# A decoder layer on one core: front-stage DMAs on other queues, larger sample loads, repeated outputs copied from scratch

## The chip, the cores and the metric

The kernel runs on 1 core of one Trainium2 chip. The metric is the device time of one execution in microseconds, the median of three runs. The engines of the core work side by side, each through its own instructions in program order: TensorE (PE in the profile), VectorE (DVE), ScalarE (ACT), GpSimd (POOL) and SyncE (SP), which only issues DMAs here. Any engine but TensorE and VectorE issues DMAs in this kernel; what it issues is carried out by 16 DMA engines.

## The reference

One layer of a decoder, run for a prompt of 1024 tokens and for 8 sequences of 4 new tokens (1056 tokens in all), width 1024, all in float32:

```python
def trunk_layer(x, h0_re, h0_im, mem_k, mem_v, attend, ...):
    q, k, v, u = jnp.split(x @ w_in, [512, 1024, 1536], axis=-1)
    o_att = attend(q, k, v)                     # 8 heads of 64, dilated windows
    y_ssm, h_re, h_im = s5_mixer(u, h0_re, h0_im, ...)   # 32 groups of 16 channels, state 64
    mixed = jnp.concatenate([rms_norm(o_att, g_att), rms_norm(y_ssm, g_ssm)], -1) @ w_out
    x = layer_norm(alpha * x + mixed, ln1_g, ln1_b)
    x = layer_norm(alpha * x + memory_attention(x, mem_k, mem_v, w_mem_q, w_mem_o), ln2_g, ln2_b)
    ffn = (jax.nn.silu(x @ w_gate) * (x @ w_up)) @ w_down       # 2816 wide
    return layer_norm(alpha * x + ffn, ln3_g, ln3_b), k, v, h_re, h_im

# s5_mixer: h[l] = abar * h[l-1] + bbar u[l];  y = Re(C h) + D u;  g = gelu(y)
#           out = g * sigmoid(g @ w_glu + b_glu)
# attend, prompt: windows (128,1), (512,4), (2048,16), combined by their denominators
# attend, sample: the same over a cache of 1024 keys and values per sequence, then the new ones
# memory_attention: 4 heads of 256 over 256 memory tokens
```

Outputs are y of both token groups, the keys and values k and v, the last SSM states, and the keys and values of the memory tokens.

## The kernel before, in words

Products are made from float32 weights as three products of a high and a low part each. A strip of weights, 128 x 1024 or 512 KB, is loaded into a buffer `wraw` (two of them) by `fetch` (line 180), ScalarE casts it to its high part `whi` (L190), and VectorE makes the low part `wlo` by subtraction (L191); `fetch` is then called for the next strip. Tokens are worked in blocks of 384, 384 and 288.

The front stage is `project`. It makes strip after strip of the input projection: first u (the SSM's input), then q, k and last v in rows of 128 tokens (`gemm_v`, L427 to L429). ScalarE copies each result from PSUM into a buffer `stg` (three of them) and stores it to scratch in DRAM: `s_u`, `s_q`, `s_k`, `s_v`. Of k and v it stores each strip twice, to scratch and to the output (`kT`, `v`; `evac_k`, `evac_v`).

Between these strips two other pieces of work are placed. `ssm()` does the SSM in two halves of 16 groups (`qf`). A half has a preparation of tables `Bs` and `CA` (L1427 to L1429, VectorE for the real and GpSimd for the imaginary parts), a load of `U` from `s_u` in eight pieces (SyncE), tap matrices that go to scratch `s_kp` (four stores on SyncE) and come back as the tile `M` (tag `ET`, eight loads on GpSimd, L1472), matmuls into `HX` (L1467), a serial scan on VectorE (L1480 to L1484), fix-ups on both engines (L1496 to L1501), output matmuls (L1511 with `M`, L1515 with `CA` and `HX`) and a gelu (L1518) into `Y`, which uses the buffer of `Bs`. GpSimd stores the state from `HX` (L1520) and SyncE stores `Y` to `s_y` in eight pieces (L1523). `sample_attn` and `sample_finish` do the attention of the new tokens: SyncE loads the caches `ckT` and `cv` in steps of four 256 KB pieces into `skv` (eight buffers, L708); VectorE and TensorE use them (L774 the values, L780 the new values).

Behind `project`, `glu` loads `s_y` as `gT` (four loads, L496) and makes the gate matmuls; the attention of the prompt loads q, k and v back from scratch (`Vn`, `Vf`). Then come the output projection, the memory attention (`evac_mem` stores each strip of memory keys and values twice, on SyncE) and the feed-forward part (`gate_up`, whose `raw` loads weights on SyncE).

`between` calls the pieces in turn, but the order of each engine's instructions is set by a list scheduler at build time, which simulates a timeline; within an engine the order is then fixed.

Of the kernel before, what the change touches and what calls it, by code (L numbers as in the profile page):

```python
# [24 lines left out]
NC = 2  # L25
MO, GU = 50, 58
# [114 lines left out]
class Body:  # L141
# [33 lines left out]
    def fetch(self):  # L175
        i = self.w_f
        if i >= self.limit or i >= len(self.rows):
            return
        r = self.t(self.wp, [128, 1024], "wraw", bufs=2)
        self.nc.scalar.dma_start(r[:], self.a["wst"][self.rows[i]])  # L180
        self.w_raw[i] = r
        self.w_f += 1
# [58 lines left out]
    def body(self, st):  # L241
        self.st = st
        tc, nc, a = self.tc, self.nc, self.a
        self._n, self._c, self.todo = 0, {}, []
        self.limit = MO

        self.rows = list(range(MO + 8)) + list(range(MO, MO + 4)) + list(range(GU, GU + 2 * NC)) + list(range(DN, a["wst"].shape[0]))
        self.w, self.w_raw, self.w_f, self.w_s = {}, {}, 0, 0
        pool = lambda name, **kw: tc.tile_pool(name=name, bufs=1, **kw)
        self.cp = st.enter_context(pool("const"))  # L250
        self.wp = st.enter_context(pool("w"))
        self.ap_ = st.enter_context(pool("act"))
        self.pp = st.enter_context(pool("ps", space=PSUM))
        self.dp = st.enter_context(pool("dram", space=bass.MemoryType.DRAM))
        self.ident = self.t(self.cp, [128, 128], "ident")
        self.ones = self.t(self.cp, [128, 128], "ones")
        self.vecs = self.t(self.cp, [128, 60], "vecs")
        nc.vector.memset(self.ones[:], 1.0 / 1024)
        self.vhalf = self.t(self.cp, [128, 8], "vhalf")
        self.vneg = self.t(self.cp, [128, 60], "vneg")  # L260
        self.phase12(st)

    def phase12(self, st):
        tc, nc, a = self.tc, self.nc, self.a
        A = [self.unit("a0"), self.unit("a1")]
        xa = lambda b, k: (A[k // 4][b][0][:, k % 4, :], A[k // 4][b][1][:, k % 4, :])
        scr = lambda name, shape: self.dp.tile(shape, F32, name=name, tag=name)
        self.s_u = scr("s_u", [512, 8 * 144])
        self.s_y = scr("s_y", [512, 8 * 136])
        self.s_kp = scr("s_kp", [2, 16, 16, 240])  # L270
        self.s_q = scr("s_q", [512, 1024])
        self.s_k = scr("s_k", [512, T])
        self.s_v = scr("s_v", [T, 512])
        self.s_mk = scr("s_mk", [128, 2048])
        self.s_mv = scr("s_mv", [128, 2048])
        self.s_z = scr("s_z", [128, 8 * T])
        self.s_x1 = scr("s_x1", [128, 8 * T])
        self.s_h = {(f, b): scr(f"s_h{f}_{b}", [128, 2 * BLK[b][1]]) for f in range(NF // 2) for b in range(3)}
        self.qs = self.t(self.cp, [128, 4, 32], "qs")
        self.ks = self.t(self.cp, [128, 4, 32], "ks")  # L280
        self.os = self.t(self.cp, [128, 4, 32], "os")
        self.qsum = self.t(self.cp, [128, 32], "qsum")
        with tc.tile_pool(name="ostage", bufs=1) as og:
            self.project(A, xa, og)
        self.rest()

    def project(self, A, xa, og):
# [3 lines left out]
        def evac_q(n, b, ps):  # L291
# [5 lines left out]
            if b == 2:  # L297
                nc.scalar.activation(self.qs[:, n, :], ps[:, 256:288], AF.Copy, scale=0.125)
            nc.scalar.dma_start(self.s_q[n * 128:(n + 1) * 128, off:off + w], r[:, :w])

        def evac_k(n, b, ps):
# [3 lines left out]
            if b == 2:  # L305
                nc.scalar.copy(self.ks[:, n, :], ps[:, 256:288])
            for o in (self.s_k, a["kT"]):
                nc.scalar.dma_start(o[n * 128:(n + 1) * 128, off:off + w], r[:, :w])

        def evac_v(r, ch, ps):  # L310
            t_ = self.t(og, [128, 384], "stg", bufs=3)
            lo, row = (0, 128 * r) if r < 8 else (96, 1024)
            nc.scalar.copy(t_[lo:, :256], ps[lo:, :256])
            for o in (a["v"], self.s_v):
                nc.scalar.dma_start(o[row:row + 128 - lo, 256 * ch:256 * ch + 256], t_[lo:, :256])

# [5 lines left out]
        with tc.tile_pool(name="ps_a", bufs=1, space=PSUM) as self.pp2, tc.tile_pool(name="ssm_small", bufs=1) as self.sp, tc.tile_pool(name="ssm_part", bufs=1) as sh, \  # L322
# [30 lines left out]
            def evac_u(n, b, ps):  # L353
# [9 lines left out]
                if b == 2:  # L363
                    for d in (u[:, 0:4, 0:8], u[:, 4:8, 136:144]):
                        nc.scalar.copy(d.rearrange("p t b -> p b t"), ps[:, 256:288].rearrange("p (b t) -> p b t", t=4))
                    nc.scalar.dma_start(self.s_u[n * 128:(n + 1) * 128, :], u[:].rearrange("p s c -> p (s c)"))

# [21 lines left out]
            for _ in ssm:  # L389
                pass  # L390
        self.nps2 = 4
        self.pp2 = self.st.enter_context(tc.tile_pool(name="ps_b", bufs=1, space=PSUM))
# [53 lines left out]
    def evac_mem(self, o1, o2, c, ps, stage):  # L446
        r = self.t(stage, [128, 512], "stg", bufs=3)
        self.nc.scalar.copy(r[:, :256], ps[:, :256])
        for o in (o1, o2):
            self.nc.sync.dma_start(o[:, c:c + 256], r[:, :256])  # L450

# [38 lines left out]
    def glu(self):  # L490
        tc, nc, a = self.tc, self.nc, self.a
        with tc.tile_pool(name="glu", bufs=1) as gp:
            G, self.mix1 = self.unit("a0"), self.unit("a1")
            gT = self.t(gp, [128, 4, 8, 136], "gT")
            for n in range(4):
                nc.sync.dma_start(gT[:, n].rearrange("p t c -> p (t c)"), self.s_y[n * 128:(n + 1) * 128, :])  # L496
            src = []
# [200 lines left out]
    def sample_attn(self, ap):  # L698
# [6 lines left out]
        def load(src, gr, c):  # L705
            t_ = [self.t(ap, [128, 512], "skv", bufs=8) for _ in range(4)]
            for b4 in range(4):
                nc.sync.dma_start(t_[b4][:], a[src][4 * gr + b4, c])  # L708
            return t_

# [31 lines left out]
    def sample_finish(self, ap, probs, load, scores, masked, tsel, bsel):  # L742
# [15 lines left out]
        for gr, (S, nm, qb) in enumerate(probs):  # L758
# [12 lines left out]
            for c in range(5):  # L771
                vt = load("cv", gr, c)
                for b4 in range(4):
                    mm(po[32 * b4:32 * b4 + 32, :], PT[:, 128 * c + 32 * b4:128 * c + 32 * b4 + 32], vt[b4][:],  # L774
                       start=c == 0, stop=False)
                yield
            vs = self.t(ap, [128, 512], "skv", bufs=8)
            nc.sync.dma_start(vs[:32], self.s_v[1024:1056, :])
# [235 lines left out]
    def raw(self, f):  # L1014
# [4 lines left out]
        for i, r in enumerate(self.raws[f]):  # L1019
            self.nc.sync.dma_start(r[:], self.a["wst"][GU + 2 * f + i])  # L1020

# [314 lines left out]
    def ssm(self):  # L1336
# [73 lines left out]
        for qf in range(2):  # L1410
# [22 lines left out]
            for i in range(8):  # L1433
                nc.sync.dma_start(U[16 * i:16 * i + 16], su[:, 16 * qf:16 * qf + 16, 7 - i, :])
            for q in range(4):
# [18 lines left out]
            for j in range(4):  # L1454
                nc.sync.dma_start(self.s_kp[qf].rearrange("h (q j) x -> h q j x", j=4)[:, :, j, :],
                                  kp[32 * j:32 * j + 16].rearrange("p q n h -> p q (n h)"))
# [13 lines left out]
            M = H("ET", (128, 16, 128))  # L1470
            for i in range(8):
                g.dma_start(M[16 * i:16 * i + 16], self.s_kp[qf, :, :, 16 * i:16 * i + 128])  # L1472
            X = HX[:, :, :, 9:137].rearrange("p g r (J j) -> p g r J j", j=8)
# [46 lines left out]
            g.dma_start(a["st"][:, gs], HX[:, :, :, 136:145])  # L1520
            sy = self.s_y[:].rearrange("(g h) (t c) -> h g t c", h=16, t=8)
            for t_ in range(8):
                nc.sync.dma_start(sy[:, 16 * qf:16 * qf + 16, t_, :], Y[16 * t_:16 * t_ + 16])  # L1523

# [15 lines left out]
```

## Time and profile before

| | |
|---|---|
| three runs | 1684.59, 1692.92, 1695.85 us; median 1692.92 |
| the profiled execution | 1688.92 us |
| its span | 1687.2 us |
| mean granted TensorE clock, share of full speed | 0.975 |
| GpSimd's queue of DMAs | 2.25 MB, 0.8% of 16 engines' span |
| SyncE's and ScalarE's queues | 137.43 MB and 59.26 MB |

The span runs from the first to the last instruction that the profiler saw. An engine's busy time holds its computing instructions, and issues of DMAs only where a row names them. In the windows PEclk is the granted clock in parts of full speed, and the DMA share is that of 16 engines; it can pass 1 a little. In timelines a row ends with the idle time before it and what released it.

### The profile page before, as it was taken

Reading aid. Unit: us, or ns where it says so; the run is one execution under the profiler, and the core shown is the slowest. Engines: PE = TensorE matmul, PEld = TensorE weight load, DVE = VectorE, ACT = ScalarE, POOL = GpSimd, SP = SyncE. Lnnn points to the kernel's source line nnn. Section 1 sums busy time; section 2 is a strip of 40 time slices with the busy share of each in tenths; the row PEclk is TensorE's granted clock in tenths of the full one; section 3 lists DMA queues with packets and bytes.
Section 4 is the critical chain, followed back from the end, with each engine's and each line's share of the span. In section 5 each row is a group of like instructions: output and inputs, shape, how many; then the busy total and the mean of one; then the engine's idle time right before and its main releaser. Section 6 shows DMA issues by size and latency. Waiting matters only on the chain.

```text
span 1687.2 us, 27817 instructions
## 1 busy us (share of the span) xinstructions
PE 1605.1 (95%) x10910; PEld 1467.3 (87%) x10910; DVE 932.5 (55%) x1785; ACT 598.9 (35%) x1164; POOL 558.2 (33%) x568
## 2 busy tenths in 40 slices
PE   7999899899999988999998999999999999999996
PEld 7998765676677977987798989999999999999995
DVE  7555554366555886235537775555555545545545
ACT  5221221465434254235514543333333333211212
POOL 3423413032222644002126555444444441000134
PEclk9999999899999998999999999999999999999998
DMA  7547967713422365126620312222222224422301
GB/s 284 131 104 193 270 155 172 247 32 112 150 71 115 101 208 203 51 83 205 234 107 26 99 66 76 76 76 78 75 81 77 76 77 148 133 77 70 115 38 66
DMA packets 97683, 200.71 MB, mean 119 GB/s; under 512 B 10384, under 2 KB 52880, under 8 KB 96784
## 3 DMA queue, kind: packets, MB, share of 16 engines
q1 hardware_dynamic: 73456, 137.43, 25.8%
q10 hardware_dynamic: 23232, 59.26, 10.9%
q0 software_dynamic: 864, 2.25, 0.8%
q8 instruction: 86, 1.41, 0.4%
q14 instruction: 45, 0.37, 0.1%
HBM read 153.85 MB, written 45.04 MB: 118 GB/s over the span
## 4 chain that ended last, share of the span: by engine, by line
PE 77%; DMA 9%; DVE 6%; ACT 3%; issue 3%; POOL 2%; SPq 1%; ACTq 0%; POOLq 0%; DVEq 0%
PE g L1052 17%; PE g L209 12%; PE g L210 12%; PE g L211 12%; PE s L1052 7%; DMA wraw<-in_wst_dram 3%; PE s L596 2%; DMA skv<-in_cv_dram 2%; PE s L598 2%; DMA skv<-in_ckT_dram 1%; POOL z L857 1%; PE g L620 1%; DVE wlo L191 1%; PE q L774 1%; DMA hr<-s_h 1%
## 5 line engine op out<-in xcount | busy, mean ns | idle before, releaser
L209 PE MATMUL g<-a0h,whi 128*128 128x384 f32 (+1 forms) x768 | 254.3, 332 | 13.6 <-ACT whi L190 8.5
L211 PE MATMUL g<-a0h,wlo 128*128 128x384 f32 (+1 forms) x768 | 250.9, 327 | 4.6 <-DVE wlo L191 4.6
L210 PE MATMUL g<-a0l,whi 128*128 128x384 f32 (+1 forms) x768 | 252.0, 328 | 0.1
L209 PE MATMUL g<-a1h,whi 128*128 128x384 f32 (+1 forms) x672 | 221.3, 329 | 0.7 <-ACT a1h L335 0.7
L210 PE MATMUL g<-a1l,whi 128*128 128x384 f32 (+1 forms) x672 | 218.2, 325 | 2.8 <-DVE a1l L337 1.8
L211 PE MATMUL g<-a1h,wlo 128*128 128x384 f32 (+1 forms) x672 | 218.5, 325 | 0.0
L209 PEld LDWEIGHTS g<-a0h,whi 128*128 128x128 f32 x768 | 147.0, 191 | 20.7 <-ACT whi L190 8.7
L190 ACT CAST whi<-wraw 128x1024 fp32r<-128x1024 f32 x84 | 88.0, 1050 | 182.9 <-PE g L210 100.9
L211 PEld LDWEIGHTS g<-a0h,wlo 128*128 128x128 f32 x768 | 147.3, 192 | 6.2 <-DVE wlo L191 5.7
L210 PEld LDWEIGHTS g<-a0l,whi 128*128 128x128 f32 x768 | 147.3, 192 | 1.9 <-DVE a0l L511 0.7
L191 DVE TENSOR_TENSOR wlo<-wraw,whi 128x1024 fp32r<-128x1024 f32 x84 | 115.0, 1371 | 47.6 <-ACT whi L190 47.4
L209 PEld LDWEIGHTS g<-a1h,whi 128*128 128x128 f32 x672 | 128.4, 191 | 5.7 <-issue 3.1
L210 PEld LDWEIGHTS g<-a1l,whi 128*128 128x128 f32 x672 | 128.3, 191 | 3.7 <-DVE a1l L337 2.0
L211 PEld LDWEIGHTS g<-a1h,wlo 128*128 128x128 f32 x672 | 128.5, 191 | 0.4 <-issue 0.2
L1045 DVE TENSOR_TENSOR wlo<-wt,wlo 128x512 fp32r<-128x512 f32 x100 | 91.0, 911 | 26.5 <-ACT wlo L1044 24.7
L1044 ACT CAST wlo<-wt 128x512 fp32r<-128x512 f32 x100 | 62.0, 620 | 110.8 <-PE g L1052 89.4
L802 DVE TENSOR_TENSOR z<-z,g 128x384 f32<-128x384 f32 (+1 forms) x96 | 49.1, 518 | 90.0 <-PE g L211 89.8
L810 POOL TENSOR_TENSOR acc<-z 128x384 f32<-128x384 f32 (+1 forms) x6 | 8.5, 1412 | 186.4 <-DVE z L802 172.7
L608 POOL TENSOR_SCALAR S<-S,rD 128x128 f32<-128x128 f32 (+7 forms) x64 | 38.0, 599 | 85.3 <-DVE rD L607 54.5
L857 POOL TENSOR_SCALAR z<-z,vneg,vecs 128x384 f32<-128x384 f32 (+1 forms) x36 | 50.3, 1410 | 44.9 <-DVE z L853 44.9
L1220 POOL TENSOR_SCALAR S<-S,rD 128x256 f32<-128x256 f32 x32 | 15.2, 478 | 111.9 <-DVE rD L1209 106.1
L596 PE MATMUL s<-K,Q 64*128 64x256 f32 (+1 forms) x128 | 42.5, 442 | 5.9 <-DVE nm L604 5.9
(459 smaller groups left out, 4031.0 us busy)
## 6 DMA issues: line engine op xcount, KB each, us to landing
wraw<-in_wst_dram ACTq DMA_DIRECT2D x88, 512.0 KB, 4.0
skv<-in_ckT_dram SPq DMA_DIRECT2D x40, 256.0 KB, 4.8
skv<-in_cv_dram SPq DMA_DIRECT2D x40, 256.0 KB, 4.9
wraw<-in_wst_dram SPq DMA_DIRECT2D x20, 512.0 KB, 4.3
wru<-in_wst_dram SPq DMA_DIRECT2D x20, 512.0 KB, 4.3
hr<-s_h SPq DMA_DIRECT2D x22, 384.0 KB, 3.4
kvm<-in_cmk_dram SPq DMA_DIRECT2D x16, 512.0 KB, 4.8
wraw<-in_cmv_dram SPq DMA_DIRECT2D x16, 512.0 KB, 4.4
```

Source lines behind the costliest of these rows:

```text
L190: self.nc.scalar.copy(h[:], r[:])
L191: self.nc.vector.tensor_tensor(out=l[:], in0=r[:], in1=h[:], op=OP.subtract)
L209: mm(out, wh, xh, start=start, stop=False)
L210: mm(out, wh, xl, start=False, stop=False)
L211: mm(out, wl, xh, start=False, stop=stop)
L596: mm(ps[:, 32 * nf:w], q, k[:, 128 * max(qt - 1, 0):128 * qt + 128], start=True, stop=True)
L608: g.tensor_scalar(out=S[:, :w], in0=S[:, :w], scalar1=rD[:], scalar2=1.0, op0=OP.mult, op1=OP.mult)
L802: self.nc.vector.tensor_tensor(out=z[:, k], in0=z[:, k], in1=ps[:, :n], op=OP.add)
L857: g.tensor_scalar(out=z[:, k], in0=z[:, k], scalar1=sc, scalar2=bi, op0=OP.mult, op1=OP.add)
L1044: act.copy(t_[:, 0], src)
L1045: v.tensor_tensor(out=t_[:, 1], in0=src, in1=t_[:, 0], op=OP.subtract)
L1052: nc.tensor.matmul(ps[:, :n], p_, q_, start=first and k + j == 0, stop=k == 3 and j == 2, skip_group_check=not first)
```

## The change

Weight strips in `project`, the stores of `s_u`, `s_q`, `s_k` and `s_v`, the loads of `U` and the stores of `s_kp` are issued by GpSimd; from the end of `project` on, weights come by ScalarE's queue as before. SyncE loads a step of a sample cache with one DMA of 1 MB into one of two buffers. `M` is loaded by one DMA with an overlapping source pattern. `s_y` has another layout in scratch, is written by one DMA per half, and `gT` is read to match. The outputs `kT`, `v`, `memkT` and `memv` are no longer stored strip by strip; SyncE copies each from scratch by one DMA while `gate_up` runs, behind a weight load of the same step.

```diff
 project, start and end:
+        self.wq = nc.gpsimd
...
+        self.wq = nc.scalar
...
 fetch:
-        self.nc.scalar.dma_start(r[:], self.a["wst"][self.rows[i]])
+        self.wq.dma_start(r[:], self.a["wst"][self.rows[i]])
...
-        self.s_y = scr("s_y", [512, 8 * 136])
+        self.s_y = scr("s_y", [2, 16, 16, 8 * 136])
...
-            nc.scalar.dma_start(self.s_q[n * 128:(n + 1) * 128, off:off + w], r[:, :w])
+            nc.gpsimd.dma_start(self.s_q[n * 128:(n + 1) * 128, off:off + w], r[:, :w])
...
-            for o in (self.s_k, a["kT"]):
-                nc.scalar.dma_start(o[n * 128:(n + 1) * 128, off:off + w], r[:, :w])
+            nc.gpsimd.dma_start(self.s_k[n * 128:(n + 1) * 128, off:off + w], r[:, :w])
...
-            for o in (a["v"], self.s_v):
-                nc.scalar.dma_start(o[row:row + 128 - lo, 256 * ch:256 * ch + 256], t_[lo:, :256])
+            nc.gpsimd.dma_start(self.s_v[row:row + 128 - lo, 256 * ch:256 * ch + 256], t_[lo:, :256])
...
 evac_mem:
-        for o in (o1, o2):
-            self.nc.sync.dma_start(o[:, c:c + 256], r[:, :256])
+        self.nc.sync.dma_start(o2[:, c:c + 256], r[:, :256])
...
 glu:
-                nc.sync.dma_start(gT[:, n].rearrange("p t c -> p (t c)"), self.s_y[n * 128:(n + 1) * 128, :])
+                nc.sync.dma_start(gT[:, n],
+                                  self.s_y[n // 2, :, 8 * (n % 2):8 * (n % 2) + 8, :].rearrange("h g x -> g h x"))
...
 sample_attn, load:
-            t_ = [self.t(ap, [128, 512], "skv", bufs=8) for _ in range(4)]
-            for b4 in range(4):
-                nc.sync.dma_start(t_[b4][:], a[src][4 * gr + b4, c])
+            t_ = self.t(ap, [128, 4, 512], "skv", bufs=2)
+            nc.sync.dma_start(t_[:], a[src][4 * gr:4 * gr + 4, c].rearrange("b p n -> p b n"))
...
 raw:
+        again = {NC + 4: ("kT", self.s_k), NC + 7: ("v", self.s_v), NC + 10: ("memkT", self.s_mk), NC + 13: ("memv", self.s_mv)}.get(f)
+        if again:
+            with self.tc.issue_after(ins.ins):
+                self.nc.sync.dma_start(self.a[again[0]], again[1][:])
...
 ssm (g is gpsimd):
-                nc.sync.dma_start(U[16 * i:16 * i + 16], su[:, 16 * qf:16 * qf + 16, 7 - i, :])
+                g.dma_start(U[16 * i:16 * i + 16], su[:, 16 * qf:16 * qf + 16, 7 - i, :])
...
-                nc.sync.dma_start(self.s_kp[qf].rearrange("h (q j) x -> h q j x", j=4)[:, :, j, :],
+                g.dma_start(self.s_kp[qf].rearrange("h (q j) x -> h q j x", j=4)[:, :, j, :],
...
-            for i in range(8):
-                g.dma_start(M[16 * i:16 * i + 16], self.s_kp[qf, :, :, 16 * i:16 * i + 128])
+            taps = self.s_kp[qf]
+            taps = bass.AP(taps.tensor, taps.offset, [[16, 8], *[list(x) for x in taps.ap[:2]], [1, 128]])
+            g.dma_start(M[:], taps)
...
-            for t_ in range(8):
-                nc.sync.dma_start(sy[:, 16 * qf:16 * qf + 16, t_, :], Y[16 * t_:16 * t_ + 16])
+            nc.sync.dma_start(self.s_y[qf].rearrange("h g (t c) -> t (h g) c", t=8), Y[:])
```

GpSimd issues 94 DMAs in the front stage where it issued 18. This is GpSimd's order at the end of the second half's preparation before; `Bs` and `CA` are the tables, `p` their factors, `sS` belongs to the sample:

```order
L1427 TENSOR_TENSOR p_260_1897<-pw_650,bb_677 128x2x128
L1428 TENSOR_TENSOR p_261_1898<-pw_650,bb_677 128x2x128
L1429 TENSOR_TENSOR Bs_1845<-p_260_1897,p_261_1898 128x2x128
L1427 TENSOR_TENSOR p_260_1897<-pw_650,bc_586 128x288
L1428 TENSOR_TENSOR p_261_1898<-pw_650,bc_586 128x288
L1429 TENSOR_TENSOR CA_1846<-p_260_1897,p_261_1898 128x2x144
L1442 MEMSET Bs_2247 128x4x112
L755 TENSOR_SCALAR sS_1533<-sS_1533,srD_2388 128x672
L755 TENSOR_SCALAR sS_1950<-sS_1950,srD_2396 128x672
L1472 DMA ET_2482<-s_kp 16x16x128 x8
```

And the same place now, where `stg` is the buffer of a row of V:

```order
L1433 TENSOR_TENSOR CA_1796<-p_241_1831,p_242_1832 128x2x144
L314 DMA s_v<-stg_2340 32x256
L1431 TENSOR_TENSOR p_245_1847<-pw_650,bb_677 128x2x128
L1432 TENSOR_TENSOR p_246_1848<-pw_650,bb_677 128x2x128
L1433 TENSOR_TENSOR Bs_1795<-p_245_1847,p_246_1848 128x2x128
L314 DMA s_v<-stg_2586 128x256
L1431 TENSOR_TENSOR p_245_1847<-pw_650,bc_586 128x288
L1432 TENSOR_TENSOR p_246_1848<-pw_650,bc_586 128x288
L1433 TENSOR_TENSOR CA_1796<-p_245_1847,p_246_1848 128x2x144
L1446 MEMSET Bs_2162 128x4x112
L314 DMA s_v<-stg_2614 128x256
L1459 DMA s_kp<-Bs_2162 64x1x240 x4
L314 DMA s_v<-stg_2661 128x256
```

Three stores of V rows stand among the preparation's rows, more behind it, and the stores of the taps follow on the same engine. SyncE's order around the first half's store of `s_y` was this, with loads of `U` for the second half in between:

```order
L708 DMA skv_2069<-in_ckT_dram 128x512
L1434 DMA U_2214<-s_u 16x16x144 x3
L1523 DMA s_y<-Bs_1775 16x16x136 x8
L1434 DMA U_2214<-s_u 16x16x144
L708 DMA skv_2126<-in_ckT_dram 128x512
L708 DMA skv_2127<-in_ckT_dram 128x512
L708 DMA skv_2128<-in_ckT_dram 128x512
L708 DMA skv_2129<-in_ckT_dram 128x512
L1434 DMA U_2214<-s_u 16x16x144 x3
L708 DMA skv_2188<-in_ckT_dram 128x512
L708 DMA skv_2189<-in_ckT_dram 128x512
L708 DMA skv_2190<-in_ckT_dram 128x512
```

And is now:

```order
L707 DMA skv_1902<-in_ckT_dram 128x4x512
L707 DMA skv_1948<-in_ckT_dram 128x4x512
L707 DMA skv_2001<-in_ckT_dram 128x4x512
L1526 DMA s_y<-Bs_1732 8x256x136
L707 DMA skv_2054<-in_ckT_dram 128x4x512
L707 DMA skv_2109<-in_ckT_dram 128x4x512
L707 DMA skv_2630<-in_cv_dram 128x4x512
```

The loads of `U` are gone from it, and a step of the cache is one row.

## Rows read from the trace of the kernel before

**Rows 1.** The page: span, and busy time of each engine with its share

```profile
span 1687.2 us, 27817 instructions
...
PE 1605.1 (95%) x10910; PEld 1467.3 (87%) x10910; DVE 932.5 (55%) x1785; ACT 598.9 (35%) x1164; POOL 558.2 (33%) x568
```

**Rows 2.** Windows of the front, one row per stretch; us

```profile
core 0: us, PE busy (x) PEld busy (x) DVE busy (x) ACT busy (x) POOL busy (x), PEclk, DMA share, GB/s
137.00:152.00 15.00, 11.86 (x114) 10.58 (x111) 12.07 (x18) 1.84 (x3) 12.58 (x16) 0.96 1.04 173
273.00:289.00 16.00, 12.87 (x69) 6.75 (x66) 9.66 (x14) 2.57 (x4) 9.62 (x13) 1.00 0.99 157
314.00:333.00 19.00, 13.21 (x84) 9.03 (x83) 8.36 (x19) 10.85 (x21) 0.67 (x2) 0.79 1.05 371
333.00:345.00 12.00, 11.92 (x50) 10.28 (x49) 5.91 (x13) 6.12 (x14) 0.98 (x3) 0.63 0.31 105
```

**Rows 3.** DMA view, 137:152, then 273:289 us: KB, us to landing

```profile
out_dram<-HX POOLq DMA_DIRECT2D x1, 72.0 KB, 13.2
...
out_dram<-HX POOLq DMA_DIRECT2D x1, 72.0 KB, 16.2
```

**Rows 4.** Chain of waits, 270 to 345 us: start, us, what

```profile
274.90 13.77 DMA skv<-in_cv_dram
...
293.41 0.66 PE s L1511 x4
294.07 0.67 PE s L1515 x8
...
299.69 0.12 PE g L428
...
303.26 0.67 ACT Bs L1518 x2
...
309.30 4.49 DMA s_y<-Bs
...
326.31 6.02 DMA wraw<-in_wst_dram
...
333.23 0.32 PE g L209
```

**Rows 5.** Timeline of GpSimd: start, us, instruction, idle before and releaser

```profile
181.57 0.74 POOL L1429 TENSOR_TENSOR Bs<-p,p 128x256 f32<-128x256 f32 x1 [10.86 <-DMA out_dram<-stg]
...
226.80 4.49 POOL L1472 DMA_DIRECT2D ET<-s_kp  x8 [10.97 <-PE s L1467]
...
269.11 1.36 POOL L1496 TENSOR_TENSOR p<-HX,qw 128x210 f32<-128x210 f32 x2 [1.28 <-DVE HX L1484]
...
282.60 0.61 POOL L1501 TENSOR_TENSOR HX<-HX,p 128x210 f32<-128x210 f32 x1
```

**Rows 6.** Timeline of VectorE inside the second half's scan

```profile
262.09 0.69 DVE L782 TENSOR_TENSOR sS<-q,sm 128x512 f32<-128x512 f32 x1 [11.31 <-PE q L780]
```

**Rows 7.** GpSimd's M loads, line 1472: ns min/median/max, first and last start

```profile
L1472 POOL DMA_DIRECT2D ET<-s_kp x16: 562/564/769, 101.5 to 230.7; - x16
```

**Rows 8.** Timeline of ScalarE: two stores of one strip

```profile
237.81 0.34 ACTq L315 DMA_DIRECT2D out_dram<-stg  x1
241.61 0.33 ACTq L315 DMA_DIRECT2D s_v<-stg  x1
```

**Rows 9.** Timeline of SyncE: the issues of the second half's s_y

```profile
303.95 6.22 SPq L1523 DMA_DIRECT2D s_y<-Bs  x8
```

**Rows 10.** DMA view of the whole run: loads of V rows

```profile
Vn<-s_v SPq DMA_DIRECT2D x4, 512.0 KB, 6.6
```

**Rows 11.** Waits, 560 to 720 us: us in total, times, longest

```profile
ACT whi L190 <- DMA wraw<-in_wst_dram: 17.5, 9, 3.6
...
ACT stg L448 <- DMA s_mv<-stg: 3.6, 1, 3.6
```

**Rows 12.** Window in the middle of gate and up

```profile
1100.00:1200.00 100.00, 100.00 (x629) 100.00 (x628) 51.23 (x72) 37.28 (x71) 46.63 (x39) 1.00 0.24 79
```

More of the change, by code (lines that the diff above doesn't have):

```diff
@@ L365, in evac_u @@
                         nc.scalar.copy(d.rearrange("p t b -> p b t"), ps[:, 256:288].rearrange("p (b t) -> p b t", t=4))
-                    nc.scalar.dma_start(self.s_u[n * 128:(n + 1) * 128, :], u[:].rearrange("p s c -> p (s c)"))
+                    nc.gpsimd.dma_start(self.s_u[n * 128:(n + 1) * 128, :], u[:].rearrange("p s c -> p (s c)"))
             self.gemm_n(0, 4, xa, evac_u, group=2)
@@ L705, in load @@
         def load(src, gr, c):
-            t_ = [self.t(ap, [128, 512], "skv", bufs=8) for _ in range(4)]
-            for b4 in range(4):
-                nc.sync.dma_start(t_[b4][:], a[src][4 * gr + b4, c])
-            return t_
+            t_ = self.t(ap, [128, 4, 512], "skv", bufs=2)
+            nc.sync.dma_start(t_[:], a[src][4 * gr:4 * gr + 4, c].rearrange("b p n -> p b n"))
+            return [t_[:, b4] for b4 in range(4)]
         def scores(o, n, q, keys):
@@ L773, in sample_finish @@
                 for b4 in range(4):
-                    mm(po[32 * b4:32 * b4 + 32, :], PT[:, 128 * c + 32 * b4:128 * c + 32 * b4 + 32], vt[b4][:],
+                    mm(po[32 * b4:32 * b4 + 32, :], PT[:, 128 * c + 32 * b4:128 * c + 32 * b4 + 32], vt[b4],
                        start=c == 0, stop=False)
                 yield
-            vs = self.t(ap, [128, 512], "skv", bufs=8)
+            vs = self.t(ap, [128, 512], "skv", bufs=2)
             nc.sync.dma_start(vs[:32], self.s_v[1024:1056, :])
@@ L1019, in raw @@
         for i, r in enumerate(self.raws[f]):
-            self.nc.sync.dma_start(r[:], self.a["wst"][GU + 2 * f + i])
+            ins = self.nc.sync.dma_start(r[:], self.a["wst"][GU + 2 * f + i])
+        again = {NC + 4: ("kT", self.s_k), NC + 7: ("v", self.s_v), NC + 10: ("memkT", self.s_mk), NC + 13: ("memv", self.s_mv)}.get(f)
+        if again:
+            with self.tc.issue_after(ins.ins):
+                self.nc.sync.dma_start(self.a[again[0]], again[1][:])
     def gate_up(self, up, X, x2):
@@ L1520, in ssm @@
             g.dma_start(a["st"][:, gs], HX[:, :, :, 136:145])
-            sy = self.s_y[:].rearrange("(g h) (t c) -> h g t c", h=16, t=8)
-            for t_ in range(8):
-                nc.sync.dma_start(sy[:, 16 * qf:16 * qf + 16, t_, :], Y[16 * t_:16 * t_ + 16])
+            nc.sync.dma_start(self.s_y[qf].rearrange("h g (t c) -> t (h g) c", t=8), Y[:])
 def kernel(**inputs):
```

## The prediction

> **What bounds the kernel now.** I read the page first: TensorE is busy 1605.1 us of the span of 1687.2 us [rows 1], so all its gaps together come to 82 us, and a change to the front stage can win no more than those that lie there. Then the windows by stage: look at the share that the DMA engines are busy beside the rate they reach. At 137 to 152 us and at 273 to 289 us the share is 1.04 and 0.99 and the rate only 173 and 157 GB/s; at 314 to 333 us the same share carries 371 GB/s [rows 2]. The DMA view names what fills the slow windows: the store of the SSM state, 72 KB in runs of 36 bytes, lands after 13.2 and 16.2 us [rows 3]. The change leaves it alone.
>
> Then the chain of waits through the second part of the front [rows 4]. It shows a sample load of the cache as a link of 13.77 us that ends at 288.7; short matmuls of the SSM; a gelu at 303.26; the store of the SSM's output s_y, landed at 313.8; the load of V; a late weight strip; and a first GLU matmul at 333.23 that takes 0.32 us, since the granted clock is 0.63 from there to 345 [rows 2, 4]. Beside it runs a serial chain: the second half of the SSM on GpSimd and VectorE. Its preparation on GpSimd starts at 181.57 after 10.86 us of idling, and GpSimd waits until 226.80 for the matmul before the scan; that is when the scan can start [rows 5]. Inside the scan VectorE, which works in program order, stands 11.31 us behind a sample matmul that had no data yet [rows 6]. The fix-ups end on GpSimd at 283.2 [rows 5].
>
> **The change part by part.** The sum is made against the profiled execution, 1688.92 us, 4 us below the median of the three runs (1692.92) and inside their spread of 11 us. A measurement of this kernel can tell about 1% from no change.
>
> (A) GpSimd issues 94 DMAs in the front where it issued 18; the 90 or so of ScalarE go. Eleven of the new ones (s_k and s_v stores, four weight strips) stand between the rows of the second half's preparation, and three more stores ahead of its M load. The only DMAs that GpSimd issues in quantity here are the M loads: 564 ns each, 769 at most, although VectorE was in its scan during the second eight [rows 7]. 11 x 0.564 = 6.2 and 3 x 0.564 = 1.7, so the scan starts 8 us later, at 235. The loads of U and the first stores fall into the idling before 181.57 and cost nothing as long as it lasts; without that cover ten issues would be 5.6 us more. From above the bound is what a store cost ScalarE: two stores of one strip went out at 237.81 and 241.61, 3.8 us apart though each is 0.34 long [rows 8]; 11 x 3.8 = 42. From below: 0, since an added issue can't shorten a chain. I take 0.564, the row of the same engine. A store now also makes GpSimd wait until ScalarE has copied its strip; queued behind it are the preparation and weight fetches, and TensorE waits for both.
>
> (B) SyncE loads each sample cache in 10 DMAs of 1 MB instead of 40 of 256 KB, and the U and s_kp transfers, with their waits, leave its queue. Sample work then reaches VectorE before the scan needs it, and the 11.31 us go. The scan took 226.8 to 269.1, 42.3 us; without the stall 31, so it ends at 266; the fix-ups, 14.1 us, with three more issues (1.7), end at 281.8 against 283.2. So A and B nearly cancel.
>
> (C) What is late next is TensorE's queue. Before, it waited for the cache until 288.7 and did the SSM's output matmuls after that, up to the gelu that ends at 303.9. Eight rounds of 0.66 and 0.67 us [rows 4] are 10.7. If the loads are in, it is free from 274.9, when that last wait began. The order puts sixty matmuls of V rows, 0.12 us each [rows 4], among the SSM's: 7.2. With 0.9 for sample and gelu 18.8, so the last gelu ends at 293.7 to 294.4; the fix-ups at 281.8 plus 10.7 and a gelu of 0.7 give 293.2, no later. Gain 9.5. If cache loads still arrive as before: 0.
>
> (D) s_y is one DMA per half for eight. Before, eight issues took 6.22 us and the last landed 9.9 us after the first began [rows 4, 9]. Lower bound 4.5, the landing of the last piece alone [rows 4]; upper 16.2, the state store [rows 3]. 512 KB of V in rows of 512 bytes land in 6.6 us [rows 10], so the 1088 KB of one half in runs of 544 bytes would by that take up to 13. Between 4.5 and 13 I take 9.9, the same: 0, with -5 to +6.
>
> (E) From s_y's landing to the first GLU matmul it was 19.4 us, at full DMA share and 371 GB/s [rows 2]. Four V rows are no longer stored twice there: 512 KB at 371 GB/s are 1.4 us; with less queued on ScalarE I take -2 (-5 to +3).
>
> (F) At the memory cross-attention sixteen 128 KB stores go from SyncE's queue. There ScalarE waited 17.5 us in nine pieces for weight strips and 3.6 us for a store buffer [rows 11]. A buffer now waits for one store, so up to 3.6 us go there; of the strips' 17.5 I take little, since they come by ScalarE's queue still. -4 (-8 to 0).
>
> (G) Four copies of about 2 MB (two) and 1 MB (two) go to gate and up. TensorE is busy 100.00 of 100 us there and the DMA share is 0.24 [rows 12]: hidden, 0; if weight strips are pushed back by a copy, up to +4.
>
> (H) At the start, weight strips and stores go by GpSimd: some twenty issues between first-half work, 0 (-1 to +2).
>
> Sum: C -9.5, D 0, E -2, F -4, G 0, H 0 is -15.5; 1688.92 - 15.5 = 1673.4. **Forecast 1673.**
>
> A rule that speaks against A: the Trainium skill, "SBUF — State Buffer", section "SBUF: two separate sides", says that GpSimd writes the descriptors of its DMAs itself and can be locked out by VectorE instructions that use the port they share, and advises ScalarE or SyncE. The issues at 564 to 769 ns beside a scan [rows 7] do not show it; by the rule, were every issue twice as long, the sum would be some 8 us worse, 1681.
>
> **Rivals.** First, slower: GpSimd becomes the bound. Mechanism: its issues block as ScalarE's two did, because the DMA engines are full or the strip is not yet copied, and the preparation of the second half stands behind them. For: GpSimd is busy 12.58 of 15 us at 137 to 152 already [rows 2], and 3.8 us lie between ScalarE's two stores [rows 8]. Against: 564 ns in [rows 7]. Price: 11 x 3.8 moves the scan from 226.8 to 268.6; plus 31, plus 14.1, plus 3 x 3.8 gives 325 for the fix-ups, then at least half the SSM rounds and a gelu, 331, where 303.9 stood; with some two V rows beside it +30; less E and F +24: **1713**. It decides from about 2 us per issue: 14 x 2 is the 28 that eat B's 11 and the slack up to the old gelu and the 6 of E and F.
>
> Second: the single transfers run on fewer DMA engines. What would do it here: s_y, the M load and the new gT source have a slowest dimension of 8 on one side where the old ones had 16 or 128. Price: twice the time of s_y, 9.9 us, for the second half at the end, and for the first half too, where GpSimd's preparation waits for tile Bs at 181.57 [rows 5], which moves the scan by as much: 1673 + 20 is about **1694**. No row of before has such a shape, so nothing there speaks for or against; the old pieces of 16 partitions landed in 4.49 us [rows 4]. The Trainium skill, "DMA: Bandwidth & Descriptors", section "Why a DMA increments its semaphore by 16 and not by 1", states that the engine count is the largest number up to 16 that divides both slowest dimensions, which would be 8 here; its sentence is all that this rival has beyond the code.
>
> Third: the change doesn't bring what it is about, as the engines, not the queues, set the pace of sample loads. For: a share of 0.99 at 157 GB/s [rows 2] while the state store is in flight, which remains; two 1 MB buffers hold no more than eight of 256 KB. Then C and B stay at 0 and A's 8 us hide behind the same wait: E and F remain, **1683**.
>
> **How the numbers follow.** Forecast 0.45, GpSimd bound 0.2, fewer engines 0.15, nothing at the loads 0.2. Bounds of the forecast: D, F, E and G low give 1673 - 5 - 4 - 3 = 1661, and B more (other stalls of ScalarE behind stores, such as the 3.8 above) another 9: 1652. High: 1673 + 6 + 4 + 5 = 1688. The range reaches up to the first rival, 1713. Faster by over 1% is below 1676: 0.6 of the forecast, a third of the third rival, a tenth of the second: 0.36. Slower by over 1%, above 1710: most of the first rival and a little of the second and forecast, 0.20. The rest 0.44.
>
> **What would show it.** In the changed kernel: GpSimd's DMA issues near 0.6 us (A right) or several us (first rival); the second scan starting near 235, with no wait of 11 us for a sample matmul (B); cache matmuls in eights instead of pairs at the end, and the last gelu near 294 (C); s_y's landing near 10 us or near 20 (D, second rival); the first GLU matmul near 322; no wait for a store buffer at 610 to 670 (F). The prediction is wrong if weight strips, now issued behind GpSimd's own work, come late and TensorE waits for the casts in the first 130 us, where I put 0, or if the clock falls for longer after a longer gap at GLU.

## The result, and the profile after

The changed kernel takes 1702.84 us (median of four runs, 1701.62 to 1704.64); the kernel before 1692.38 beside it. The ratio is 1.0073, interval 1.005 to 1.0096: slower by 0.7%, where 1673 was forecast. Its page, to set against [rows 1]:

```profile
span 1700.1 us, 27627 instructions
...
PE 1582.1 (93%) x10910; PEld 1461.4 (86%) x10910; DVE 932.8 (55%) x1785; ACT 599.3 (35%) x1164; POOL 593.8 (35%) x644
```

TensorE is busy 23 us less and the span is 13 us longer. Where it arises is seen at the first matmul of the memory projection; first before, then after (line, engine, operation: ns min/median/max, first and last start):

```profile
L209 PE MATMUL g<-mm,whi x64: 280/283/574, 581.3 to 605.9; 128*128 128x256 f32 x64
```

```profile
L209 PE MATMUL g<-mm,whi x64: 280/283/574, 594.9 to 619.5; 128*128 128x256 f32 x64
```

The front is 13.6 us late. From there to the end it was 1687.2 - 581.3 = 1105.9 us and is 1700.1 - 594.9 = 1105.2: the rest of the kernel gave nothing. In the front, SyncE's timeline around the two stores of s_y [rows 9]:

```profile
166.06 0.77 SPq L1526 DMA_DIRECT2D s_y<-Bs  x1
...
316.49 0.60 SPq L1526 DMA_DIRECT2D s_y<-Bs  x1
332.15 0.35 SPq L560 DMA_DIRECT2D mask<-in_mask_p_dram  x1
...
336.15 3.21 SPq L495 DMA_DIRECT2D gT<-s_y  x2
```

The second store is issued in 0.60 us, and the mask's load, which comes when it has landed, starts at 332.15: 15.7 us, where 9.9 were taken [rows 4, 9]. The windows of the changed kernel, columns as in [rows 2], show what the DMA engines did in that time:

```profile
317.00:332.00 15.00, 0.00 (x0) 0.00 (x0) 1.23 (x1) 0.67 (x2) 0.54 (x1) 0.65 0.50 142
332.00:345.00 13.00, 5.82 (x34) 4.20 (x35) 1.33 (x9) 2.76 (x7) 1.21 (x3) 0.50 0.92 243
```

In the first window the share is 0.50 and TensorE has no matmul. Only two weight strips of 512 KB and 128 KB of V are on their way beside the store. Before, the tail ran at 1.05 and 371 GB/s [rows 2]. From 332 on the granted clock is 0.50, the 1.2 GHz level, after TensorE had no matmul for 15 us. GpSimd's timeline, against [rows 5]:

```profile
184.97 0.99 POOL L1433 TENSOR_TENSOR Bs<-p,p 128x256 f32<-128x256 f32 x1 [13.85 <-DMA s_y<-Bs]
...
192.54 0.57 POOL L180 DMA_DIRECT2D wraw<-in_wst_dram  x1 [3.75 <-DVE wlo L191]
...
198.31 0.57 POOL L180 DMA_DIRECT2D wraw<-in_wst_dram  x1 [2.59 <-DVE wlo L191]
...
204.57 0.57 POOL L180 DMA_DIRECT2D wraw<-in_wst_dram  x1 [3.04 <-DVE wlo L191]
...
240.98 1.90 POOL L1477 DMA_DIRECT2D ET<-s_kp  x1 [1.18 <-PE s L1471]
...
282.24 1.77 POOL L1501 TENSOR_TENSOR p<-HX,qw 128x210 f32<-128x210 f32 x2
```

The second preparation starts at 184.97, after s_y of the first half, issued at 166.06, has landed 18.9 us later. (That store was not alone: from 166 to 175 us, beside loads of the cache and of `U` and stores of `s_k`, the share is 1.10 at 191 GB/s.) Inside it three weight fetches wait 3.75, 2.59 and 3.04 us for VectorE to free a buffer; the scan begins near 241, not 226.8, and the fix-ups at 282.24, not 269.1. ScalarE's and TensorE's timelines of the end:

```profile
306.89 1.67 ACT L510 CAST a0h<-gT 128x384 fp32r<-128x384 f32 x2 [9.64 <-DMA gT<-s_y]
308.46 0.90 ACT L1523 ACTIVATE Bs<-s 128x408 f32<-128x408 f32 x2
...
315.78 0.69 ACT L1523 ACTIVATE Bs<-s 128x272 f32<-128x272 f32 x2 [1.01 <-DVE wlo L191]
...
348.49 2.40 ACT L510 CAST a0h<-gT 128x384 fp32r<-128x384 f32 x4 [6.14 <-DMA gT<-s_y]
```

```profile
339.18 2.47 PE L596 MATMUL s<-K,Q 64*128 64x128 f32 x10 [22.55 <-DMA gT<-s_y]
```

ScalarE stands 9.64 us at a cast of gT, whose load has the new shape, with a gelu of the SSM queued behind the cast; the last gelu comes at 315.78, not 303.26 [rows 4]. TensorE then stands 22.55 us, and the second pair of gT, issued at 336.15, is cast at 348.49. While the first pair of gT is nearly all that is in flight, the share is again near one half (columns as above):

```profile
299.50:307.00 7.50, 7.12 (x61) 6.15 (x59) 0.00 (x0) 0.11 (x1) 0.00 (x0) 1.00 0.46 108
```

### The profile page after: what moved, and what is told of

It is laid out like the page before. It is cut to its first block, busy times and chain, and to the rows that moved or that the text cites. A ratio compares the mean times of both kernels' runs of the same rounds, so it can differ in the third digit from the quotient of the medians.

```text
span 1700.1 us, 27627 instructions
## 1 busy us (share of the span) xinstructions
PE 1582.1 (93%) x10910; PEld 1461.4 (86%) x10910; DVE 932.8 (55%) x1785; ACT 599.3 (35%) x1164; POOL 593.8 (35%) x644
## 5 line engine op out<-in xcount | busy, mean ns | idle before, releaser
L209 PE MATMUL g<-a0h,whi 128*128 128x384 f32 (+1 forms) x768 | 254.9, 333 | 21.0 <-ACT whi L190 10.7
L596 PE MATMUL s<-K,Q 64*128 64x256 f32 (+1 forms) x128 | 40.8, 434 | 24.6 <-DMA gT<-s_y 22.5
```

Of the source, the lines that this page charges most:

```text
L209: mm(out, wh, xh, start=start, stop=False)
L596: mm(ps[:, 32 * nf:w], q, k[:, 128 * max(qt - 1, 0):128 * qt + 128], start=True, stop=True)
```

## The experiments

Theory S: the transfers with a slowest dimension of 8 (the s_y store, gT, M) move on half of the DMA engines, and their late landings make the loss. Theory G, the first rival: GpSimd, waiting in program order, is what is late. All times below are medians; ratios are against the kernel before, run on the same chip.

**s_y and gT as before.** The edit on the changed kernel, and the second one, on weights:

```diff
 a1_sy_back
-            nc.sync.dma_start(self.s_y[qf].rearrange("h g (t c) -> t (h g) c", t=8), Y[:])
+            for t_ in range(8):
+                nc.sync.dma_start(sy[:, 16 * qf:16 * qf + 16, t_, :], Y[16 * t_:16 * t_ + 16])
 (and s_y [512, 8 * 136], gT read by rows)
 a2_w_scalar
-        self.wq = nc.gpsimd
+        self.wq = nc.scalar
 a3_both: both;  b1_sy_alone: the new s_y and gT on the kernel before
```

> The changed kernel with s_y and gT as before: eight stores per half from 16 partitions, gT read as rows. Theory S (the single store of s_y, and gT, move on half of the DMA engines: in the changed kernel 1088 KB took 18.9 us from issue to landing for the first half and 15.7 for the second, with a DMA share of 0.51 while little else was in flight): the first half's lands about 10 us after its first issue, so the second preparation starts 8 us earlier, the second lands 6 us earlier and gT's second pair 5: 1685 to 1692. Theory G (GpSimd's waits in program order, for weight buffers and strips, are what made the second half late): the preparation still takes 36 us, and the time stays within 3 us of the changed kernel, 1700 to 1703.

> The changed kernel with the weight strips of the front issued by ScalarE. Theory G: the three waits for the buffer of a strip between rows of the second preparation (3.75, 2.59 and 3.04 us) go from GpSimd's queue, the preparation takes 27 us for 36.6, and the time falls by about 9 to 1694. Theory S: nothing that sets the end is touched; within 3 us of 1702.8, since the time gained waits for s_y and gT.

> Both undone: s_y and gT as before, weights by ScalarE. If S and G each hold and add, 1702.8 - 14 - 9 = about 1680, below the kernel before; if only S holds, as with s_y alone (1685 to 1692); if only G, 1694.

> The kernel before with only the new s_y: another layout, one store per half, gT to match. Theory S: each store lands 15 to 19 us after its issue for 10, the second preparation starts 8 us later and the tail is 6 to 10 us longer: 1702 to 1710. Theory G: s_y costs nothing by itself, 1690 to 1694.

Measured: a1 1684.22 us (0.9978, 0.9966 to 0.9991); a2 1701.33 (1.0085, 1.006 to 1.011); a3 1689.04 (1.0008, 0.9988 to 1.0028); b1 1709.51 (1.0124, 1.0094 to 1.0155), beside 1687.82 before. S's range holds b1, and a1 lies 0.8 us below its range; G fails on a2. Weights on ScalarE gave nothing, and a3 is no better than a1. In a2 GpSimd's preparation takes 30 us (184.34 to 214.30) and not 36, and the time stays. Its timelines of GpSimd and ScalarE show where the gain goes:

```profile
271.56 1.37 POOL L1501 TENSOR_TENSOR p<-HX,qw 128x210 f32<-128x210 f32 x2 [3.16 <-DVE HX L1489]
```

```profile
311.65 0.94 ACT L510 CAST a0h<-gT 128x384 fp32r<-128x384 f32 x1 [6.51 <-DMA gT<-s_y]
312.49 0.68 ACT L1523 ACTIVATE Bs<-s 128x272 f32<-128x272 f32 x2
```

The fix-ups start 10.7 us earlier than in the changed kernel (271.56 for 282.24), but the last gelu stands behind a cast that waits for gT, and comes only 3.3 us earlier (312.49 for 315.78).

**Which part of S.** The load alone, then the store as well:

```diff
 c2_gt_pieces
-                nc.sync.dma_start(gT[:, n], self.s_y[n // 2, :, 8 * (n % 2):8 * (n % 2) + 8, :].rearrange("h g x -> g h x"))
+                for g8 in range(8):
+                    nc.sync.dma_start(gT[16 * g8:16 * g8 + 16, n], self.s_y[n // 2, :, 8 * (n % 2) + g8, :])
 c4_rows (gT in pieces of the new layout)
-        self.s_y = scr("s_y", [2, 16, 16, 8 * 136])
+        self.s_y = scr("s_y", [2, 128, 16, 144])
-            nc.sync.dma_start(self.s_y[qf].rearrange("h g (t c) -> t (h g) c", t=8), Y[:])
+            nc.sync.dma_start(self.s_y[qf, :, :, :136], Y[:])
```

> The changed kernel with gT loaded in 32 pieces of 16 partitions for 4 loads, runs of 4352 bytes as in the changed kernel; s_y is stored as there. If the shape of gT's load carries a good part of the 18.6 us between the changed kernel and the one with s_y as before, the second pair of gT lands some 5 us earlier and the time is 1694 to 1698, less what 14 more issues per pair cost SyncE (0.35 us each, 5 us); if the store carries it, 1700 to 1706.

> As the last one, gT in 32 pieces (here with runs of 544 bytes), but the store of s_y has a row of scratch for each partition, padded so that its runs stay 544 bytes: still one DMA per half, with a slowest dimension of 2048 for 8. Theory S: it lands 7 to 9 us after its issue instead of 15 to 19, and the time is about 10 us below the last one, near 1692. Rival N: it lands as late as in the changed kernel and the time agrees with the last one.

Measured: c2 1694.02 (1.0036, 1.002 to 1.0053), c4 1682.06 (0.9967, 0.9953 to 0.9982), beside 1687.34. So loading gT in pieces is worth 6 us, and the store's layout 12. The first step changes the number of gT's loads with their shape, and no run parts the two; for the shape speaks the share of 0.46 above. The second step also shortens the runs of gT's loads, to 544 bytes. Both kernels store 1088 KB with one DMA in runs of 544 bytes; SyncE's timelines, c2 and then c4:

```profile
307.31 0.63 SPq L1526 DMA_DIRECT2D s_y<-Bs  x1
322.98 0.36 SPq L560 DMA_DIRECT2D mask<-in_mask_p_dram  x1
```

```profile
307.95 0.55 SPq L1526 DMA_DIRECT2D s_y<-Bs  x1
315.10 0.36 SPq L560 DMA_DIRECT2D mask<-in_mask_p_dram  x1
```

15.7 us and 7.2 us to the next row, which waits for the landing. Their windows in between, c2 and then c4, columns as above:

```profile
308.00:322.90 14.90, 1.75 (x8) 0.94 (x6) 3.63 (x5) 2.89 (x6) 0.54 (x1) 0.65 0.50 143
```

```profile
308.50:315.00 6.50, 1.89 (x8) 0.95 (x6) 3.61 (x5) 3.02 (x6) 0.54 (x1) 0.79 1.01 294
```

Twice the share and twice the rate, with nothing changed but the scratch's layout; beside the store two weight strips and 128 KB of V are on their way in both. So one DMA for eight is not what is slow (rival N fails).

**The shape by itself.** Extra DMAs in gate and up:

```diff
+        if f in (NC + 5, NC + 11):
+            self.nc.sync.dma_start(self.p8[:, :112, :136], r[:, :952].rearrange("p (g c) -> p g c", c=136))
+        if f in (NC + 8, NC + 14):
+            self.nc.sync.dma_start(self.p128[:, :, :136], r[:, :952].rearrange("p (g c) -> p g c", c=136))
 (p8 is [8, 113, 144], p128 is [128, 7, 144]; the reads of s_y likewise)
```

> The changed kernel with extra DMAs on SyncE in the middle of gate and up, where the DMA share is 0.32: 476 KB of a weight buffer stored in runs of 544 bytes, once with a destination whose slowest dimension is 8 (the shape of the new s_y store) and once with 896; and 512 KB read from s_y into a weight buffer ahead of its strip in runs of 4 KB, once grouped 8 by 16 as the new gT load and once as 128 rows. The values are overwritten or not read. Theory S (the slowest dimension of 8 puts the transfer on 8 engines): the first of each pair takes about twice as long from issue to landing, 6 to 9 us against 3 to 5. Rival N (a single large DMA is slow whatever its shape, eight in flight are what made the old store quick): the two of each pair agree within 20%.

The DMA view of 8 us around each store, 40 slices of 0.2 us; the digits are tenths of the 16 engines. First the slowest dimension of 8, then 896:

```profile
DMA  1100000000014444444545555555553100000000
GB/s 82 41 20 0 0 0 0 0 0 0 0 41 103 95 92 92 84 84 120 128 131 141 152 152 166 158 139 136 150 141 82 44 5 0 0 0 0 0 0 0
```

```profile
DMA  0000000009999999800000000000000000000000
GB/s 0 0 0 0 0 0 0 0 22 286 307 313 307 307 310 307 259 19 0 0 0 0 0 0 0 0 0 0 0 0 0 0 0 0 0 0 0 0 0 0
```

The first moves for some 20 slices, 4 us, at four to five tenths and 80 to 170 GB/s; the second for 9 slices, 1.8 us, at nine tenths and 300. By these rates 1088 KB alone would move in about 9 and 4 us (an estimate: times 1088/476); 15.7 and 7.2 were measured for c2 and c4 from the store's issue to the next row, with other transfers in flight. The reads of s_y in runs of 4 KB went out among weight loads and could not be told apart from them. The run itself, 1707.55 us, carries extra work and says nothing.

**What remains of the change.** From a1, first the queues and the load size:

```diff
 a4_scalar_all (a3, and for s_u, s_q, s_k, s_v)
-            nc.gpsimd.dma_start(self.s_k[...
+            nc.scalar.dma_start(self.s_k[...
 a5_skv4 (a1, and skv in four pieces of 256 KB, bufs=8)
 a6_rows_scalar: c4, with the edits of a4
```

> The changed kernel with s_y and gT as before, and the weight strips and the stores of u, q, k and v issued by ScalarE; what remains of the change are the loads of 1 MB, U, s_kp and M on GpSimd and the four copies. If GpSimd's queue is what gave the 3.6 us by which the variant with s_y as before beats the kernel before, this gives them back: 1688 to 1692, as the one with only the weights on ScalarE did (1689). If single stores and copies gave them: 1682 to 1685.

> The changed kernel with s_y and gT as before (1684), and the caches loaded in pieces of 256 KB into eight buffers. If the loads of 1 MB are worth something with the other queues as changed, 1689 to 1694; if not, 1682 to 1686.

> The single s_y store by rows (slowest dimension 2048) with gT in pieces, and weights and stores of u, q, k and v on ScalarE. Each of the two changes gave 1682 by itself where the kernel before took 1687. If they work on different waits (the landing of s_y, 7 us for 10; and GpSimd's issues in the preparation), they add: 1677 to 1680. If the tail behind s_y takes back what comes earlier, 1682.

Measured: a4 1682.29 (0.9957, 0.9937 to 0.9977), a5 1692.53 (1.0015, 0.9996 to 1.0034), a6 1679.06 (0.9944, 0.9926 to 0.9962). GpSimd's queue gave nothing that can be measured: without its stores and weights the kernel is 0.2% better, less than the intervals of a1 and a4 can separate (they overlap from 0.9966 to 0.9977). Loads of 1 MB are worth 0.4% even here.

Then single edits on the kernel before:

```diff
 b2_copies: stores to scratch only, and the four copies in raw
 b3_copies_1mb: b2, and
+            t_ = self.t(ap, [128, 4, 512], "skv", bufs=2)
+            nc.sync.dma_start(t_[:], a[src][4 * gr:4 * gr + 4, c].rearrange("b p n -> p b n"))
 d1_m_single: b3, and M in one load;  d2_u_skp: b3, and U and s_kp on GpSimd
 d3_1mb_only: the loads of 1 MB alone;  d4_b3_rows: b3, and s_y and gT as in c4
```

> The kernel before with the four outputs stored once, to scratch, and copied in gate and up; nothing else changed. If the double stores cost time in the front and the memory stage (terms E and F, 2 and 4 us), 1681 to 1684 where the kernel before takes 1687; if the DMA engines hide them, 1686 to 1689.

> As the last one, and the caches loaded by DMAs of 1 MB (two buffers). If loads of 1 MB free the queue of SyncE and bring the last gelu forward (terms B and C, up to 9.5 us), 5 to 10 us below the last one; if the DMA engines set the pace of the loads (third rival), within 2 us of it.

> Copies and 1 MB loads on top of the kernel before (1670), and M in one load with a slowest dimension of 8. If M's shape carries the missing 12 us (it takes half of the engines and lands late, and the loads of the cache beside it come later), 1680 to 1683; if not, 1669 to 1672.

> Copies and 1 MB loads on top of the kernel before (1670), and U and s_kp issued by GpSimd. If these carry the 12 us (five us more in the preparation of the second half, where TensorE waits for its tables, and a scan that starts five us later), 1678 to 1683; if not, 1669 to 1672.

> The kernel before with loads of 1 MB alone; outputs stored twice as before. If the copies have no part, as their variant alone suggests (1688.7 for 1689.3), 1669 to 1673; if the double stores fill the DMA engines beside the loads, 1674 to 1680.

> Copies, 1 MB loads and the single s_y store by rows with gT in pieces. If the store's 3 us add, 1666 to 1668; if the 28 more loads of gT on SyncE take them back, 1669 to 1673.

Measured: b2 1688.69 (0.9998, 0.9977 to 1.0018); b3 1669.94 (0.9888, 0.9866 to 0.991); d1 1674.62 (0.9918, 0.9902 to 0.9935); d2 1675.81 (0.9928, 0.9913 to 0.9943); d3 1678.84 (0.9937, 0.9913 to 0.996); d4 1672.04 (0.9905, 0.9889 to 0.9921). **b3 beats both kernels**, by 19 us and 31 us (ratios 0.9888 to 1, and to 1.0073); it lies 19 us below b2, where 5 to 10 were expected. d1 and d2 fall between their two ranges: each carries a part of the missing time. d4 gains nothing over b3. b3's timelines of SyncE, GpSimd and VectorE show the prediction's steps B and C:

```profile
287.07 6.42 SPq L1524 DMA_DIRECT2D s_y<-Bs  x8
```

```profile
175.26 0.90 POOL L1430 TENSOR_TENSOR Bs<-p,p 128x256 f32<-128x256 f32 x1 [11.22 <-DMA U<-s_u]
...
195.91 0.47 POOL L1443 MEMSET Bs<- 128x448 f32 x1 [0.18 <-PE s L1439]
...
217.68 4.49 POOL L1473 DMA_DIRECT2D ET<-s_kp  x8 [10.81 <-PE s L1468]
...
252.26 1.37 POOL L1497 TENSOR_TENSOR p<-HX,qw 128x210 f32<-128x210 f32 x2 [1.18 <-DVE HX L1485]
```

```profile
244.75 0.69 DVE L778 TENSOR_TENSOR sS<-q,sm 128x512 f32<-128x512 f32 x1 [3.50 <-PE q L776]
```

The wait inside the scan is 3.50 us for 11.31 [rows 6], the fix-ups start at 252.26 for 269.11 [rows 5], and s_y goes out at 287.07 for 303.95 [rows 9]. TensorE no longer lacks cache data in the first pass either: 126 to 165 us, before, then b3, then d3, which has the loads of 1 MB and still stores the outputs twice (its profile is of the slowest of its ten runs):

```profile
126.00:165.00 39.00, 35.86 (x330) 31.53 (x322) 22.71 (x85) 4.59 (x8) 15.32 (x19) 0.96 0.81 207
```

```profile
126.00:165.00 39.00, 39.00 (x381) 34.39 (x380) 22.28 (x81) 6.08 (x12) 15.68 (x21) 1.00 0.77 202
```

```profile
126.00:165.00 39.00, 34.09 (x298) 30.25 (x289) 23.08 (x88) 4.59 (x8) 15.32 (x19) 0.83 0.81 209
```

In b2, with the copies alone, TensorE is busy 35.79 of these 39 us. Of these four profiles only the one with both edits has the first pass full.

M in one load costs about 0.3% (the intervals of d1 and b3 overlap a little), and it lands late. The DMA view of d1 at 217 to 245 us, then of b3, and TensorE's wait in each:

```profile
ET<-s_kp POOLq DMA_DIRECT2D x1, 1024.0 KB, 19.2
```

```profile
ET<-s_kp POOLq DMA_DIRECT2D x8, 128.0 KB, 8.5
```

```profile
241.68 1.94 PE L770 MATMUL q<-skv,qb 128*32 128x512 f32 x8 [8.22 <-DMA skv<-in_cv_dram]
```

```profile
230.14 1.93 PE L770 MATMUL q<-skv,qb 128*32 128x512 f32 x8 [3.86 <-DMA skv<-in_cv_dram]
```

The one load lands 19.2 us after its issue; the eight take 8.5 us each (the median) and go out over 4.49 us. TensorE waits 4.4 us more for the next cache load. U and s_kp on GpSimd cost 0.4%; its timeline in d2, against 195.91 above:

```profile
206.06 0.47 POOL L1443 MEMSET Bs<- 128x448 f32 x1 [5.78 <-PE s L1439]
```

GpSimd waits 5.78 us for a transpose. That U's loads come late behind other work on its queue is argued, not tried apart from s_kp. The copies alone do nothing and the loads alone 0.6%, together 1.1%. The first pass above speaks for the two working together, but that isn't settled: the intervals of d3 and b3 lie close (0.9913 and 0.991), and the runs of d3 spread over 16 us.

## Why the prediction was wrong

**The step that failed is D**, with the load of gT that the sum didn't cost. D took the single store at 9.9 us, as eight took. It was 18.9 and 15.7, and its layout decides: 12 us of the time from the store (c2 to c4), 6 from the load (changed kernel to c2). I had the mechanism as the second rival at 0.15 and 1694. Its price of 20 left out gT, and I let it weigh little because no row showed such a shape, though the outer dimension of 8 stood in the code. The Trainium skill, "DMA: Bandwidth & Descriptors", section "Why a DMA increments its semaphore by 16 and not by 1", gives 8 engines for this store; the trace agrees, with four to five tenths of the 16 engines busy in the experiment with extra DMAs, where the store is alone. The range of 1652 to 1713 holds the measured 1702.84 only because it reaches up to the first rival, GpSimd as the bound, and a2 and a4 speak against that one: this is luck.

**A** had its price right and missed its waits. The issues of weights and of V rows on GpSimd (ns min/median/max, first and last start):

```profile
L180 POOL DMA_DIRECT2D wraw<-in_wst_dram x20: 531/545/727, 1.3 to 257.2; - x20
```

```profile
L314 POOL DMA_DIRECT2D s_v<-stg x18: 518/552/591, 210.0 to 318.0; - x18
```

Over 160 to 300 us of the changed kernel GpSimd waits (us in total, times, longest):

```profile
POOL s_v L314 <- ACT stg L313: 31.1, 10, 5.8
POOL wraw L180 <- DVE wlo L191: 16.7, 5, 6.8
```

From the first table to the memset behind the preparation it is 36.1 us (184.97 to 221.09), where it was 22.5 (181.57 to 204.06). But these waits set little of the end: weights and stores back on ScalarE are worth some 3.5 us (a1 to a4, 0.9978 to 0.9957), which the intervals don't separate from nothing. The second zero that failed is that of M, U and s_kp, which A counted at nothing or B gave to SyncE as a relief: they cost 5 us (M, d1) and 7 us (U and s_kp, d2) by the ratios. In the changed kernel TensorE stands 10.0 us for the M tile, a wait that the kernel before doesn't have (us in total, times, longest, 100 to 350 us):

```profile
PE s L1516 <- DMA ET<-s_kp: 10.0, 1, 10.0
```

The rule of the Trainium skill, "SBUF — State Buffer", section "SBUF: two separate sides", that the prediction weighed against A (VectorE locks GpSimd out of writing descriptors) was not seen to act: none of the issues of weights and of V rows took over 727 ns.

**B and C** were right in mechanism and too small: the loads of 1 MB with the copies give 19 us, of which 16.9 show at the issue of s_y in b3. In the changed kernel the last gelu came 12.5 us later than before, instead of 9.5 earlier: the second half started late, and a cast of gT stood ahead of the gelus. In a2 the second half came 10.7 us earlier and moved the gelu by only 3.3, with the cast ahead of it. The third rival (the engines set the pace, and the loads bring nothing) falls with d3 and b3, though the loads of 1 MB alone gave only half of what they gave with single stores.

**E** starts from a matmul that is the first of the GLU on the chain, but not the first of the GLU; that one ran at 317.64. Before, TensorE and then ScalarE with the second pair of gT:

```profile
317.64 0.34 PE L209 MATMUL g<-a0h,whi 128*128 128x384 f32 x1
```

```profile
332.45 2.40 ACT L510 CAST a0h<-gT 128x384 fp32r<-128x384 f32 x4
```

From the landing of s_y to the cast of the second pair it was 18.6 us (313.87 to 332.45) and is 16.3 (332.15 to 348.49), near the -2 of E; what is late is the landing. **F** was -4 and is nothing: ScalarE's wait for the store buffer is gone and that for weight strips is 10.9 us for 17.5 [rows 11], yet the stage from the memory projection to the end is only 0.7 us shorter, and b2, with the copies and single stores alone, is 0.9998. That list still names 23.7 us of ScalarE behind TensorE, where it was 23.6.

```profile
ACT whi L190 <- DMA wraw<-in_wst_dram: 10.9, 8, 2.8
```

**G** was right: the copies land in 8 to 12 us, and in the window of one of them TensorE is busy all the time, as in [rows 12].

```profile
1112.00:1212.00 100.00, 100.00 (x629) 100.00 (x628) 51.26 (x72) 37.32 (x71) 46.69 (x39) 1.00 0.32 111
```

**The sum by measured pieces**, as ratios: b3 0.9888; M in one load +0.0030; U and s_kp on GpSimd +0.0040; together 0.9958, and a4, which holds just these, is 0.9957. Stores and weights on GpSimd +0.0021 (a1), the new s_y and gT +0.0095 (changed kernel). So the change holds a gain of 19 us and losses of 31. Each of these steps is uncertain by 0.2 to 0.3% (the two intervals that it is taken from), so the agreement to 0.0001 is partly luck, and of the losses only that of s_y and gT is well clear of noise. What the cast ahead of the gelu costs by itself was not tried.

## What to carry to other kernels

When eight small DMAs are joined into one, look at the slowest dimension of both sides as well as at the bytes: here it fell from 16 to 8, the one transfer was slower than the eight, and it showed as a DMA share near one half while little else was in flight. A bundle of edits should be costed edit by edit, with every transfer whose shape changes, readers of a new scratch layout included. A queue that is moved to a computing engine brings its waits with it, but only an experiment tells which of them sets the end.

## What the runs showed of the hardware that was not expected

- The same 1088 KB in the same runs of 544 bytes, in one DMA, each beside two weight strips and 128 KB of V: 15.7 us at a share of 0.50 with a slowest dimension of 8, 7.2 us at 1.01 with 2048.
- Ten loads of 1 MB for each cache instead of forty of 256 KB, with the same buffer space, and outputs stored once kept TensorE busy 39.00 of 39 us in the first pass for 35.86, although the DMA share there is 0.77 for 0.81. Neither edit did so alone: 34.09 with the loads (d3, its slowest run), 35.79 with the single stores (b2).
